# Two due steps of the attention heads for one weight piece, in a two-layer hybrid trunk

## The chip, the cores and the metric

One Trainium2 chip, one core. The metric is the device time of one execution in microseconds (us), the median of several runs; lower is better. PE is TensorE, DVE is VectorE, ACT is ScalarE, POOL is GpSimd, SP is SyncE, which here only issues DMAs.

## What is computed

Two layers over a sequence of 256 frames of width 2048, all in float32. Each layer projects `x` with one wide matrix, feeds three groups of heads, gates them, and maps them back:

```python
def hybrid_layer(x, mem, w_in, rel_table, gate_w, gate_b, gla_norm_g, w_mem_kv, w_out, ln_g, ln_b):
    h = x @ w_in
    a_q, a_k, a_v, a_z, b_q, b_k, b_v, b_z, b_lr, m_q, m_z = jnp.split(h, cuts, axis=-1)
    y_a = chunk_band_attention(a_q, a_k, a_v, rel_table)      # 8 heads of 128, own chunk of 64 and 8 before
    log_g = jax.nn.log_sigmoid(b_lr @ gate_w + gate_b) / GATE_TAU
    o_b = gla_chunk_recurrence(b_q, b_k, b_v, log_g)          # 4 heads, gated linear attention
    o_b = o_b * lax.rsqrt(mean(o_b ** 2) + RMS_EPS) * gla_norm_g
    mk, mv = jnp.split(mem @ w_mem_kv, 2, axis=-1)
    y_m = memory_attention(m_q, mk, mv)                       # 4 heads into 256 memory tokens
    y = jnp.concatenate([y_a * silu(a_z), o_b * silu(b_z), y_m * silu(m_z)], axis=-1)
    return layer_norm(DEEPNORM_ALPHA * x + y @ w_out, ln_g, ln_b)
```

## The kernel before

**The weight stream.** Nearly all the work is the product of the 256 frames with the weights, which are streamed once from HBM. A product of 512 output columns is a group (`as_group`, L266) of eight weight *pieces*, each of 256 rows. A piece (`piece`, L140) is loaded by SP into `raw`; ACT casts it to `wh` (L128) and DVE forms the rest `wl` (L129), four buffers of each; PE then makes 12 matmuls of a piece into the tile `acc`: `xh*wh`, `xl*wh`, `xh*wl` for two blocks of rows and two of frames. Groups come in this order in a layer: (MV, MK), BQK, two groups of values (512 and 264 columns), AQ0, AK0, values (512), AQ1, AK1, values (264), MQ, BZ, AZ0, AZ1, MZ, and four of the output projection (WO0 and WO1 in turns, WO2, WO3).

**The steps beside it.** The heads are Python generators whose `yield n` means "not before `n` more ticks". After each piece `tick` (L52) moves the clock on by the piece's width (1 for 512 columns, 0.516 for 264) and decides what is issued behind that piece. It first runs all due entries of `side` (reads back of turned tiles, splits, gating), and then works on `active`: up to two head generators while the recurrence `gla` runs, up to three afterwards, drawn from `waiting`. A generator that ends does not count; one that yields again ends the tick. `finish` ticks on, without weight pieces, until given generators are done.

- `gla` (L306): the linear attention of one layer, thirteen steps, the only one of its kind.
- `a_head` (L540), heads a0 to a7: first step two score matmuls into a bank of PSUM, softmax on DVE (`L547`, `L552`, `L555`, `L557`) and ACT (`L554`), turning by `turned`; `yield 9`; second step the products with the values (from `asv`), copy to `yraw` by ACT (`L590`); `yield 2`; end. Heads 0 to 3 also load the bias of head h + 4 in the second step. For heads 0, 1 and 7 the turned scores `pT` and the values are first split into two parts (`split`, on ACT and DVE), into tiles whose buffers carry the tags `gq` or `gk` and `pairs0` or `pairs1`; the tiles `yT` of `gla_turned` use `gq` and `gk` too.
- `m_head` (L593), heads m0 to m3: scores against the memory keys, softmax (`L607`, `L608`, `L611` to `L614`), turning; `yield 10`; split of `pT`; `yield 2`; products with the values; `yield 2`; end.
- `turned` (L520): DVE transposes blocks into a scratch tile, POOL stores it in DRAM (`home`, L527), and two ticks later POOL issues four reads back (L532).
- `gated` (L499): when all heads of a group are done, their outputs are multiplied with the SiLU gate and split, as an operand of the output projection.

PE, SP and POOL issue in the order in which the program is written, so the tick decides what stands between which pieces in their queues. On DVE and ACT the order is set when the program is built, by a list scheduler with priorities (the weight casts and `wl` go ahead by a high priority) and a model of the times; `placed_here` pins an instruction behind the one written before it on its engine. PSUM has four banks for the steps (`bank`), the scratch pool has eight tiles.

Of the kernel before, what the change touches and what calls it, by code (L numbers as in the profile page):

```python
# [36 lines left out]
def hybrid_trunk_kernel(  # L37
# [14 lines left out]
    def tick(share=1.0):  # L52

        now[0] += share
        for e in [e for e in side if e[1] <= now[0]]:
            side.remove(e)
            after = next(e[0], None)
            if after is not None:
                side.append((e[0], now[0] + after))
            else:  # L60
                done.add(e[0])
        while True:
            while waiting and len(active) < (3 if all(g in done for g in linear) else 2):
                active.append((waiting.pop(0), 0))
            due = [e for e in active if e[1] <= now[0]]
            if not due:
                return
            active.remove(due[0])
            g = due[0][0]
            after = next(g, None)  # L70
            if after is not None:
                active.append((g, now[0] + after))
                return
            done.add(g)

    def finish(gens):
        while not all(g in done for g in gens):
            tick()
# [187 lines left out]
    def as_group(src, xq, n, kp=2, first=None, need={}):  # L266

        acc = psd.tile([P, 2, 512], F32, name=nm("acc"), tag="acc")
        for pc in range(16 // kp):
            if first is not None and pc % 2 == 0:  # L270
                xq.append(load_quarter(first[pc // 2]))
            finish(need.get(pc, ()))
            w = piece(src[pc], n, kp)
            for kk in range(kp):
                for t in range(2):
                    as_products(acc[:, t, :n], t, xq, w, pc * kp + kk, kk)
            tick(n / 512)
        return acc
# [558 lines left out]
    for l in range(L):  # L837
# [176 lines left out]
        for n in range(WO_N):  # L1014
# [35 lines left out]
            for m, pc in order:  # L1050
                finish(need.pop(pc, ()))
                w = piece(wo_pieces(l, m)[pc], 512)
                for kk in range(2):
                    for t in range(2):
                        as_products(accs[m][:, t], t, yq, w, pc * 2 + kk, kk)
                tick()
                if pc == 7:
                    for t in range(2):
                        add_residual(m, t, accs[m][:, t], stats)
                    if last:  # L1060
                        r = res[:, 1, columns(m)]
                        dve.tensor_tensor(r, r, gb[m][0], op=ALU.mult)
# [97 lines left out]
```

## Time and profile before

| | |
|---|---|
| median of 3 runs | 897.69 us (896.99 to 899.18) |
| span of the profiled execution | 896.4 us, 13888 instructions; it is this span that stands for the profiled execution's own time |
| PE busy | 887.2 us, 99% |
| DVE, ACT, POOL busy | 617.4 us, 482.1 us, 231.0 us |
| granted PE clock | 0.997 on average |
| DMA | 216.90 MB, mean 242 GB/s |

Times within the profile are counted from the span's start. A row of the chain has start, duration, engine, output tile and line; a row of a timeline has the engine, the line, the operation, the tiles and shapes, and in brackets the idle time of the engine before it with what ended it. Rows of matmuls that overlap give the time from the first start to the last modelled end. A row of windows gives the busy time of PE, PE's weight load, DVE, ACT and POOL, the granted clock, the share of the DMA engines and GB/s. In a row of waits stand the total, the number and the longest.

### The profile page before, as it was taken

How to read it: one execution, taken by the hardware profiler on the slowest of the kernel's cores; microseconds unless marked ns; L12 is line 12 of the kernel's file. 1: busy time of each engine (PE TensorE's matmuls, PEld its weight loads, DVE VectorE, ACT ScalarE, POOL GpSimd, SP SyncE). 2: the span in 40 equal slices, each digit the busy share in tenths (PEclk: the TensorE clock that was granted, in tenths of full speed). 3: DMA queues.
4: the chain of work that ended last, by engine and by line, in shares of the span. 5: the costliest groups of instructions: out<-in, count | busy, mean ns of one | idle time of the engine just before them, and what ended most of it. 6: DMA issues, size and time to landing. Idle time of an engine off the chain costs nothing.

```text
span 896.4 us, 13888 instructions
## 1 busy us (share of the span) xinstructions
PE 887.2 (99%) x4669; PEld 743.5 (83%) x4669; DVE 617.4 (69%) x905; ACT 482.1 (54%) x698; POOL 231.0 (26%) x431
## 2 busy tenths in 40 slices
PE   9999999999999999999999999999999999999996
PEld 7878988888988888888888888888888888888885
DVE  6756568767467676665595786896664758676866
ACT  6644475555446575543465545754754557565440
POOL 0022103114305353410034230231061444432300
PEclk9999999999999999999999999999999999999998
DMA  9988779867979797975689968696589897979752
GB/s 310 312 241 245 215 245 265 275 197 225 275 253 241 236 274 236 307 241 193 224 267 268 265 195 282 201 287 210 154 234 293 242 260 236 276 222 281 223 179 95
DMA packets 166088, 216.90 MB, mean 242 GB/s; under 512 B 25232, under 2 KB 143376, under 8 KB 166016
## 3 DMA queue, kind: packets, MB, share of 16 engines
q1 hardware_dynamic: 148256, 173.29, 63.7%
q0 software_dynamic: 17472, 42.33, 16.4%
q8 instruction: 37, 0.61, 0.3%
q10 hardware_dynamic: 288, 0.39, 0.1%
q14 instruction: 35, 0.29, 0.1%
HBM read 194.78 MB, written 21.10 MB: 241 GB/s over the span
## 4 chain that ended last, share of the span: by engine, by line
PE 98%; DVE 1%; DMA 0%; ACT 0%; issue 0%; SPq 0%; DVEq 0%
PE acc L102 91%; PE bk L102 6%; DMA raw<-w 0%; ACT wh L128 0%; DVE mv L129 0%; ACT res L823 0%; DVE wl L129 0%; PE bk L665 0%; DVE stats L809 0%; DVE res L808 0%; SPq L201 0%; DVE res L759 0%; SPq L179 0%; DVE mvt L762 0%; PE bk L812 0%
## 5 line engine op out<-in xcount | busy, mean ns | idle before, releaser
L102 PE MATMUL acc<-wh,x 128*128 128x512 f32 (+2 forms) x2516 | 747.8, 381 | 1.3 <-DVE mv L129 0.7
L102 PEld LDWEIGHTS acc<-wh,x 128*128 128x128 f32 x2516 | 460.6, 188 | 88.2 <-PE acc L102 1.1
L129 DVE TENSOR_TENSOR wl<-raw,wh 128x1024 fp32r<-128x1024 f32 (+3 forms) x321 | 368.4, 1152 | 198.9 <-ACT wh L128 187.0
L128 ACT CAST wh<-raw 128x1024 fp32r<-128x1024 f32 (+3 forms) x321 | 318.5, 996 | 344.2 <-PE acc L102 201.7
L102 PE MATMUL acc<-wl,x 128*128 128x512 f32 (+2 forms) x1258 | 475.9, 379 | 0.0
L102 PEld LDWEIGHTS acc<-wl,x 128*128 128x128 f32 x1258 | 236.0, 188 | 45.3 <-DVE wl L129 0.4
L527 POOL DMA_DIRECT2D home<-sc x76 | 42.5, 560 | 426.2 <-DVE sc L525 417.6
L532 POOL DMA_DIRECT2D pT<-home x96 | 52.4, 552 | 30.2 <-DMA home<-sc 12.1
L532 POOL DMA_DIRECT2D qk<-home x64 | 34.9, 553 | 36.5 <-DMA home<-sc 26.2
L532 POOL DMA_DIRECT2D zT<-home x48 | 26.2, 551 | 20.5 <-DMA home<-sc 14.0
L525 DVE STREAM_TRANSPOSE sc<-sc 128x512 f32<-128x512 f32 (+1 forms) x38 | 24.9, 668 | 3.7 <-ACT sc L996 3.0
L532 POOL DMA_DIRECT2D yr<-home x48 | 26.3, 557 | 3.2 <-DMA home<-sc 3.2
L525 DVE STREAM_TRANSPOSE sc<-acc 128x512 f32<-128x512 f32 x28 | 18.3, 691 | 4.3 <-PE acc L102 4.3
L554 ACT ACTIVATE sc<-sc,mx 128x128 f32<-128x128 f32 (+1 forms) x32 | 14.3, 448 | 8.9 <-DVE mx L552 8.8
L547 DVE SCALAR_TENSOR_TENSOR sc<-bk,bias 128x384 f32<-128x384 f32 x16 | 8.6, 539 | 10.7 <-PE bk L102 10.7
L128 ACT CAST x<-sc 128x512 fp32r<-128x512 f32 x20 | 12.2, 617 | 5.2 <-DVE sc L508 3.2
L532 POOL DMA_DIRECT2D xT<-home x24 | 13.2, 552 | 6.9 <-DMA xT<-home 5.2
L129 DVE TENSOR_TENSOR x<-sc,x 128x512 fp32r<-128x512 f32 x20 | 13.5, 685 | 1.4 <-ACT x L128 1.4
L102 PE MATMUL bk<-qk,qk 128*128 128x128 f32 (+1 forms) x64 | 13.1, 326 | 0.0
L698 DVE SCALAR_TENSOR_TENSOR res<-res,acc 128x512 f32<-128x512 f32 x15 | 9.7, 682 | 4.7 <-PE acc L102 4.7
L532 POOL DMA_DIRECT2D yT<-home x16 | 8.8, 555 | 14.8 <-DMA home<-sc 14.8
L129 DVE TENSOR_TENSOR x<-res,x 128x512 fp32r<-128x512 f32 (+2 forms) x13 | 10.0, 790 | 2.0 <-ACT x L128 2.0
(210 smaller groups left out, 524.3 us busy)
## 6 DMA issues: line engine op xcount, KB each, us to landing
raw<-w SPq DMA_DIRECT2D x387, 256.0 KB, 4.6
raw<-w SPq DMA_DIRECT2D x62, 512.0 KB, 5.0
home<-sc POOLq DMA_DIRECT2D x60, 256.0 KB, 4.4
raw<-w SPq DMA_DIRECT2D x32, 388.0 KB, 5.1
raw<-w SPq DMA_DIRECT2D x32, 264.0 KB, 3.5
qk<-home POOLq DMA_DIRECT2D x64, 64.0 KB, 4.7
raw<-w SPq DMA_DIRECT2D x32, 124.0 KB, 4.8
bias<-relw SPq DMA_DIRECT2D x16, 192.0 KB, 4.4
```

The lines of the kernel that those rows point to most:

```text
L102: pe.matmul(o, l, r, start=start, stop=stop, skip_group_check=True)
L128: keep(act.copy(hi, src))
L129: keep(dve.tensor_tensor(lo, src, hi.bitcast(F32), op=ALU.subtract))
L525: dve.transpose(blocks.rearrange(order, j=32), src.rearrange("p (g b j) -> p g b j", b=4, j=32))
L527: pool.dma_start(homes[-1], blocks)
L532: pool.dma_start(dst[b * 32:(b + 1) * 32], home[:, b].rearrange("(a i) n -> i a n", a=4))
L547: dve.scalar_tensor_tensor(s, pb[:, :384], SCALE, bias[h], op0=ALU.mult, op1=ALU.add)
L554: act.activation(s[:, own[t]], s[:, own[t]], AF.Exp, bias=mx[:, t:t + 1], accum_out=zs[:, t:t + 1])
L698: dve.scalar_tensor_tensor(r, r, ALPHA, acc, op0=ALU.mult, op1=ALU.add)
```

## The change

In `tick`, a head step that yields again no longer ends the tick; the second one does.

```diff
             else:
                 done.add(e[0])
+        steps = 0
         while True:
             while waiting and len(active) < (3 if all(g in done for g in linear) else 2):
                 active.append((waiting.pop(0), 0))
...
             after = next(g, None)
             if after is not None:
                 active.append((g, now[0] + after))
-                return
+                steps += 1
+                if steps == 2:
+                    return
+                continue
             done.add(g)
```

The limits of `active`, all due times, the weight pieces and the work of every step stay as they are.

## The prediction

> **What bounds the kernel now.** I read the page first (engine shares, slices, the chain that ended last), then the waits of TensorE (PE), then the chain piece by piece, and only then the clock times of single heads.
>
> ```profile
> PE 887.2 (99%) x4669; PEld 743.5 (83%) x4669; DVE 617.4 (69%) x905; ACT 482.1 (54%) x698; POOL 231.0 (26%) x431
> PE   9999999999999999999999999999999999999996
> PEclk9999999999999999999999999999999999999998
> PE acc L102 91%; PE bk L102 6%; DMA raw<-w 0%; ACT wh L128 0%; DVE mv L129 0%; ACT res L823 0%; DVE wl L129 0%; PE bk L665 0%; DVE stats L809 0%; DVE res L808 0%; SPq L201 0%; DVE res L759 0%; SPq L179 0%; DVE mvt L762 0%; PE bk L812 0%
> ...
> PE bk L102 <- DVE eps L836: 1.1, 1, 1.1
> PE bk L812 <- DVE nt L777: 0.9, 1, 0.9
> PE acc L102 <- DVE mv L129: 0.7, 1, 0.7
> PE acc L102 <- ACT wh L128: 0.7, 2, 0.3
> PE bk L102 <- ACT nparts L813: 0.3, 1, 0.3
> ```
>
> The chain is PE for 97%: 91% weight products (acc), 6% matmuls of the heads and the transposes (bk). The second block is every wait of PE: 3.7 us in all, and by the names they lie at the start (eps, mv) and in the last normalization (nt, nparts); none belongs to a head. So where the change acts PE never waits, at full clock. In such a kernel a new order gains only what a change-over between two kinds of matmul costs, and loses whatever makes PE wait.
>
> ```profile
> 240.90 21.80 PE acc L102 x96
> 262.69 0.66 PE bk L102 x4
> ...
> 292.64 0.65 PE bk L102 x4
> 293.29 2.75 PE acc L102 x12
> 296.05 0.65 PE bk L102 x4
> ```
>
> The chain in order of time (start, duration). Eight pieces without a step take 21.80 us: 2.725 us a piece, 0.227 us a matmul. With a step between, a piece and its step take 296.05 - 292.64 = 3.41 us: 0.65 the step's own four matmuls, 0.035 the change-over.
>
> **The change part by part.** *Which ticks change.* I counted through the ticks by the yields (9 and 2 in an attention head; 10, 2, 2 in a memory head; the recurrence's own list), with one step and with two. They differ, in each layer, in six ticks that now let two through: scores of a1 and a2 behind AQ1's last piece; products with the values ("values" below) of a1 and a2 behind the second 264-column piece; scores of a4 and a5 (BZ, first piece); values of a4 and a5 (AZ0, second); scores of a7 and m0 (AZ0, fourth); m1's split and m2's scores (AZ1, seventh). Of these the first five put two matmul groups side by side. What follows moves up too: a5 and a6 by one piece, a7 by one, m0 and m1 by two, m2 by five, m3 by three, the last gating by two. The recurrence is due alone at its ticks, and no loop of empty ticks gets shorter.
>
> *PE's own work.* No matmul is added or taken. Ten pairs (five in each of two layers) save at most one change-over each: 10 x 0.035 = 0.35 us, at least nothing. I take 0.2, between the two.
>
> *First scores, SP and the banks.* The 16 bias loads stay; a2's second load (for a6) is issued two short pieces earlier, 192 KB that then stand ahead of two weight loads in SP's queue. Weights have their smallest reserve just behind that place:
>
> ```profile
> 234.11 1.23 DVE L129 TENSOR_TENSOR wl<-raw,wh 128x1024 fp32r<-128x1024 f32 x1 [1.83 <-ACT wh L128]
> 237.80 0.40 PE L102 MATMUL acc<-wl,x 128*128 128x512 f32 x1
> 220.00:242.00 22.00, 22.00 (x148) 20.39 (x147) 10.60 (x15) 10.62 (x17) 12.05 (x23) 1.00 0.94 273
> ```
>
> The rest of a weight piece is ready at 235.34 and used at 237.80: 2.46 us. 192 KB at the 273 GB/s of that stage are 0.70 us. Cost 0 under that cover; without it up to 0.7 us a layer.
>
> *a2, a5, a6.* Their values come up to two short pieces (a matmul of 264 columns by 0.227 x 264/512 = 0.117, so 2 x 12 x 0.117 = 2.8 us) or one long one earlier, but their scores move up as well.
>
> ```profile
> 223.39 1.18 POOL L532 DMA_DIRECT2D pT<-home  x2 [0.62 <-DMA yr<-home]
> DMA to landing us min/median/max: 3.4/4.3/5.7
> 230.82 0.81 PE L102 MATMUL bk<-pT,asv 128*128 128x256 f32 x4
> ```
>
> The middle row is the time from issue to landing of the pT reads of that stage (min, median, max). a2's last read is issued at about 224.0 and lands by 228.3 (median) to 229.7; PE needs it at 230.82, afterwards at 228.0. On POOL the order becomes home a1, home a2, reads a1, reads a2, then eight reads for the queries (AQ1), which today stand ahead of a2's and take 4.4 us: a2 gains more than the 2.8 it loses. The query reads are late by a2's four (2.2 us), with eight pieces of cover. Cost 0.
>
> *m0 and m1 scores* at about 297.3 and 300.8 need the memory queries:
>
> ```profile
> 280.44 0.69 DVE L129 TENSOR_TENSOR mq<-yr,mq 128x512 fp32r<-128x512 f32 x1
> 302.71 0.76 PE L102 MATMUL bk<-mk,mq 128*128 128x256 f32 x5
> 303.32 2.26 POOL L532 DMA_DIRECT2D yT<-home  x4 [4.28 <-DMA home<-sc]
> 310.77 0.56 POOL L527 DMA_DIRECT2D home<-sc  x1 [4.64 <-DVE sc L525]
> ```
>
> Ready at 281.1: cover 16 us. But m0's store (home), 8.1 us after its scores today, now stands on POOL ahead of the reads of yT, the recurrence's output: these go from 303.3 to about 305.9 and are used by ACT at 317.86 (below). Even landing 5.7 us late they have over 4 us left. Cost 0.
>
> *a7's values* are the tight place.
>
> ```profile
> 317.86 1.28 ACT L495 ACTIVATE x<-yT,ng 128x128 fp32r<-128x128 f32 x4
> 319.15 1.13 DVE L496 SCALAR_TENSOR_TENSOR x<-yT,ng,x 128x128 fp32r<-128x128 f32 x4
> 320.31 0.41 ACT L128 CAST sc<-pT 128x256 fp32r<-128x256 f32 x1 [0.23 <-DVE x L496]
> 322.30 0.71 ACT L128 CAST sc<-pT 128x256 fp32r<-128x256 f32 x2 [0.43 <-DMA pT<-home]
> 321.67 0.28 DVE L129 TENSOR_TENSOR sc<-asv,sc 128x128 fp32r<-128x128 f32 x1
> 321.90 1.23 DVE L129 TENSOR_TENSOR wl<-raw,wh 128x1024 fp32r<-128x1024 f32 x1
> 323.05 0.76 DVE L129 TENSOR_TENSOR sc<-pT,sc 128x256 fp32r<-128x256 f32 x2
> 325.99 0.52 PE L102 MATMUL bk<-sc,sc 128*128 128x256 f32 x3
> 765.94 0.52 PE L102 MATMUL bk<-sc,sc 128*128 128x256 f32 x3
> ```
>
> a7's split shares a buffer (tag gk) with yT, so it starts only when VectorE (DVE) has done with yT at 320.28, whatever its due time, and ends at 321.95. PE uses it at 325.99 today, at 325.99 - 2.72 = 323.27 afterwards: the reserve falls from 4.0 to 1.3 us. (The last row is the same step in layer 1, 439.95 us on.) m0's split moves up two pieces and could come first: 0.71 on ACT, 0.76 on DVE. That still fits. Cost 0; at the other end one weight piece gets ahead on DVE as well, 0.76 + 1.23 - 1.32 = 0.7 us a layer. I take 0, nearer to the order of today's rows.
>
> The Trainium skill, TensorE: Matmul & The Clock Gate, section on engine queue depths, says that matmuls stay in program order and that ScalarE and VectorE are strict FIFO. It speaks against the change: a step let through before its data is there holds up every weight piece behind it. Here that would be the whole 0.7 us a layer, since the trace has no idle PE time in which to make it good; in today's order no step of a head shows it.
>
> *m1's values.*
>
> ```profile
> 332.97 1.08 ACT L996 ACTIVATE sc<-acc 128x512 f32<-128x512 f32 x2
> 333.94 0.71 ACT L128 CAST sc<-pT 128x256 fp32r<-128x256 f32 x2
> 335.47 0.72 DVE L129 TENSOR_TENSOR sc<-pT,sc 128x256 fp32r<-128x256 f32 x2
> 340.98 0.89 PE L102 MATMUL bk<-sc,mv 128*128 128x256 f32 x6
> 347.37 1.28 ACT L611 ACT_TABLE_LOAD   x1 [1.83 <-DVE mx L608]
> ```
>
> m1's split ends at 336.19, PE uses it at 340.98: 4.8 us. Afterwards two pieces less and m2's scores more (0.72) precede: 340.98 - 5.44 + 0.72 = 336.26. Its reads and its split are issued two pieces (5.4 us) earlier as well, so the reserve stays if the split keeps its distance to its reads. If it stays behind AZ1's SiLU (332.97, itself 0.72 later) there is none: rival two. m2 and m3 give their values in WO with the same 12 ticks after their scores as now. I take 0.
>
> *Sum.* Against the profiled span of 896.4: -0.2 + 0 = 896.2. The runs are 896.99, 897.69 and 899.18; the median is 1.3 us above that span. Forecast 897.69 - 0.2 = 897.5, no change. A measurement of this kernel tells about 0.3%, 2.7 us, from none.
>
> **The rivals.** *One: a7's split is late.* 0.7 us in each layer gives 897.5 + 1.4 = 898.9. For it: a reserve of 1.3 us, and ACT and DVE are busiest just there. Against: m0's split alone does not fill it. It would pass 0.3% only at 1.4 us a layer, two more weight pieces.
>
> *Two, slower: m1's split stays behind the SiLU.* m2's exponentials now fall ahead of that SiLU, so ScalarE must load the exponential's table and then the SiLU's again. Split ended at 336.19 + 0.72 = 336.91 against a need of 336.26: 0.65 us late with no load, 1.93 with one of 1.28, 3.2 with two. At two layers 1.3, 3.9 or 6.4 us: 898.8, 901.4, 903.9; with one load the middle, 901.4. It decides from one load on. For it: the split stands behind the SiLU today although its reads were issued by 322.4. Against: it is two pieces earlier in program order, and ACT has idle time before the SiLU.
>
> The Trainium skill, ScalarE: Activation LUTs, section on what a table load costs, gives about 1283 ns and a drain of some 1380 ns for each switch. The trace agrees on the load, 1.28 us; no row here prices the drain. By the page's total a late split with one load costs an estimated 2 x 1.38 = 2.8 us more, 904.2.
>
> *Three, faster: side by side the second group hides under the first.* If all of it went, 10 x 0.65 = 6.5 us, 891.2. Against: the 96 plain matmuls above are neighbours of one kind already and still take 0.227 us each; neighbours do not hide under one another.
>
> *Four: the change does nothing.* Only 12 ticks let two through; the time is then 897.7, inside the forecast.
>
> **How the numbers follow.** Forecast (with four) 0.63, rival one 0.21, two 0.13, three 0.03. Predicted 897.5. From 896.3 (0.35 saved, the lower runs' 0.7 below the median, a little over) to 901.5 (rival two with one load); outside lie rival three and the upper part of two, together with mixtures no more than 2 in 10. The forecast's own range is 896.3 to 899.2. Faster by over 0.3%: rival three, 0.03. Slower: most of two and 0.01 of one, 0.11. Within: 0.86.
>
> **What would show it.** Right: no wait of PE on a head's split, pT or mq; busy PE near 887 us; in the chain ten pairs of head steps as one entry of about 1.3 us; a7's values near 323.3 and 763.2 with idle PE ahead of them at most some tenths. Wrong: a wait "PE bk L102 <- DVE sc L129" (rival one near 323 and 763, two near 336 and 776), more than today's table loads, or a wait of PE on wl or wh near 237. A reordering of casts by the planner elsewhere, which the rows of before can't show, would also make it wrong.

## The result and the profile after

The changed kernel takes 900.8 us (median), the kernel before, beside it, 898.08 us: ratio 1.003, interval 1.0022 to 1.0039. It is slower by 2.7 us; the forecast was no change. Measured again beside other experiments, it gave 1.0031 (1.0019 to 1.0043). Each ratio here is taken against the kernel before as run beside it (its median there 897.87 to 898.29 us) and is not exactly the quotient of the medians. One of the twelve executions with only the pairs of a4 and a5 took 1275.73 us at a mean clock of 0.655; that run's numbers are given without it.

The profiled execution (902.17 us, span 900.3) is the second longest of thirteen; one part of its loss is not usual, as an experiment shows below. The page's row of engines and the first row of PE's waits after the change:

```profile
PE 890.2 (99%) x4669; PEld 745.0 (83%) x4669; DVE 616.4 (68%) x905; ACT 488.2 (54%) x702; POOL 231.7 (26%) x431
PE bk L106 <- DMA pT<-home: 2.6, 3, 1.4
```

(Line numbers are four higher than before.) The wait is new: 2.6 us in all, three times, 1.4 the longest, on `pT`, the turned scores that a head reads back from DRAM. None of the waits that the rivals named is there. PE's timeline around the values of a4 and a5 shows where, first before the change (layer 0), then after it (two rows of each layer); the brackets hold the idle time ahead of a row:

```profile
289.07 0.81 PE L102 MATMUL bk<-pT,asv 128*128 128x256 f32 x4
292.48 0.81 PE L102 MATMUL bk<-pT,asv 128*128 128x256 f32 x4
```

```profile
288.60 0.81 PE L106 MATMUL bk<-pT,asv 128*128 128x256 f32 x4
290.24 0.89 PE L106 MATMUL bk<-pT,asv 128*128 128x256 f32 x4 [0.83 <-DMA pT<-home]
...
729.97 0.89 PE L106 MATMUL bk<-pT,asv 128*128 128x256 f32 x4 [0.35 <-DMA pT<-home]
732.24 1.31 PE L106 MATMUL bk<-pT,asv 128*128 128x256 f32 x4 [1.39 <-DMA pT<-home]
```

a5's values now stand directly behind a4's, at 289.2 and not 3.41 us later, and its turned scores are not there: 0.83 us in layer 0, 1.39 in layer 1, where a4's are late as well (0.35). POOL's timeline of the same stretch says why: first before the change, then after it. A row is a run of transfers that POOL issues; `home` is a head's store to DRAM, `yr` the eight reads for the memory queries (MQ), `pT` the reads of turned scores.

```profile
267.99 0.54 POOL L527 DMA_DIRECT2D home<-sc  x1 [5.81 <-DVE sc L525]
268.54 4.45 POOL L532 DMA_DIRECT2D yr<-home  x8
273.24 0.56 POOL L527 DMA_DIRECT2D home<-sc  x1 [0.25 <-DVE sc L525]
273.80 0.55 POOL L532 DMA_DIRECT2D pT<-home  x1
275.40 1.69 POOL L532 DMA_DIRECT2D pT<-home  x3 [1.05 <-DMA yr<-home]
277.08 0.56 POOL L527 DMA_DIRECT2D home<-sc  x1
279.43 2.17 POOL L532 DMA_DIRECT2D pT<-home  x4 [1.79 <-DMA home<-sc]
```

```profile
267.54 0.54 POOL L531 DMA_DIRECT2D home<-sc  x1 [5.81 <-DVE sc L529]
273.45 0.54 POOL L531 DMA_DIRECT2D home<-sc  x1 [5.37 <-DVE sc L529]
274.02 4.37 POOL L536 DMA_DIRECT2D yr<-home  x8
278.89 0.56 POOL L531 DMA_DIRECT2D home<-sc  x1 [0.51 <-DMA yr<-home]
279.45 1.10 POOL L536 DMA_DIRECT2D pT<-home  x2
281.05 2.26 POOL L536 DMA_DIRECT2D pT<-home  x4 [0.50 <-DMA yr<-home]
283.88 1.64 POOL L536 DMA_DIRECT2D pT<-home  x3 [0.58 <-DMA yr<-home]
285.78 0.55 POOL L536 DMA_DIRECT2D pT<-home  x1 [0.26 <-DMA pT<-home]
287.27 1.09 POOL L536 DMA_DIRECT2D pT<-home  x2 [0.94 <-DMA pT<-home]
```

Before, POOL used the time between a4's store and a5's store for the MQ reads. Now a5's scores stand behind the same weight piece as a4's, so in program order a5's store comes directly behind a4's, ahead of the MQ reads. The store is not earlier for it: DVE still works through a4's softmax before a5's, and a5's store starts at 273.45 (273.24 before). DVE's first instruction on a5's scores shows it; it starts when a4's are turned:

```profile
266.67 0.58 DVE L529 STREAM_TRANSPOSE sc<-sc 128x384 f32<-128x384 f32 x1
267.17 0.52 DVE L551 SCALAR_TENSOR_TENSOR sc<-bk,bias 128x384 f32<-128x384 f32 x1
```

So POOL stands 5.37 us, and then issues all it has in one burst. a4's four reads end up 5 us later (279.45 to 281.6 for 273.80 to 276.5).

The reserve of a5 in layer 0 can be worked out from these rows and one of the chain after the change, which follows the wait back to the transfer:

```profile
284.42 5.68 DMA pT<-home
290.10 0.14 issue
290.24 0.89 PE bk L106 x4
...
719.75 6.21 DMA home<-sc
725.97 0.28 issue
726.25 5.86 DMA pT<-home
732.11 0.14 issue
732.24 1.31 PE bk L106 x4
733.55 3.95 PE acc L106 x12
```

Before, a5's fourth read was issued at 279.43 + 3 x 0.54 = 281.05 and landed at 286.33 by the record of its semaphore; PE used it at 292.48: a reserve of 6.15 us. After, it goes out at 284.42 and lands at 290.10, 3.77 us later (3.37 by the issue, 0.40 by a slower landing). PE would use it 0.65 us behind the start of a4's values, at 289.25, which is 3.23 us earlier. 6.15 - 3.77 - 3.23 = -0.85 us; the idle time measured is 0.83.

In layer 1 the last row shows a second effect: twelve matmuls in 3.95 us, which normally take 2.75. The windows of that stretch (length, busy PE, PEld, DVE, ACT and POOL with the number of their instructions, the granted clock, the share of the DMA engines, GB/s):

```profile
732.00:734.00 2.00, 1.76 (x6) 1.58 (x7) 0.39 (x1) 0.37 (x1) 0.77 (x2) 0.64 0.77 202
734.00:736.00 2.00, 2.00 (x6) 1.52 (x6) 0.00 (x0) 0.00 (x0) 0.00 (x0) 0.51 0.83 277
```

PE, idle for 1.7 us between 729.6 and 732.2, got half the clock afterwards; the clock records of the trace put it at 732.57 to 735.98, 3.41 us, which is 1.7 us of work. Waits of 2.6 and 1.7 make 4.3 us; the spans differ by 3.9.

### The profile page after: what moved, and what is told of

The parts are those of the page before. It is cut to its first block, busy times and chain, and to the rows that moved or that the text cites. A ratio compares the mean times of both kernels' runs of the same rounds, so it can differ in the third digit from the quotient of the medians.

```text
span 900.3 us, 13883 instructions
## 1 busy us (share of the span) xinstructions
PE 890.2 (99%) x4669; PEld 745.0 (83%) x4669; DVE 616.4 (68%) x905; ACT 488.2 (54%) x702; POOL 231.7 (26%) x431
## 4 chain that ended last, share of the span: by engine, by line
PE 81%; issue 9%; DMA 6%; POOL 2%; DVE 1%; ACT 0%; POOLq 0%; ACTq 0%
PE acc L106 76%; PE bk L106 5%; DMA home<-sc 2%; DMA qk<-home 1%; DMA pT<-home 1%; POOL pT L536 1%; POOL yr L536 1%; DMA yr<-home 1%; POOL home L531 0%; DMA raw<-w 0%; POOL kdT L536 0%; ACT wh L132 0%; DVE wl L133 0%; ACT res L827 0%; PE bk L669 0%
## 5 line engine op out<-in xcount | busy, mean ns | idle before, releaser
L106 PE MATMUL bk<-pT,asv 128*128 128x128 f32 (+1 forms) x52 | 10.8, 328 | 2.6 <-DMA pT<-home 2.6
L106 PEld LDWEIGHTS bk<-pT,asv 128*128 128x128 f32 x52 | 9.1, 194 | 4.3 <-issue 2.3
```

Of the source, the lines that this page charges most:

```text
L106: pe.matmul(o, l, r, start=start, stop=stop, skip_group_check=True)
```

## The experiments

The theory: the six ticks of the prediction are harmless but for the group a4, a5, a6. Scores of a4 and a5 behind one piece bring POOL into the worse order, values of a4 and a5 behind one piece need the result earlier, and only together do they use up the reserve. Rivals: another pair costs the time; one of the two halves alone is enough; the half clock is the loss, not the wait.

**One step per piece in BZ alone.** With the scores of a4 and a5 their values too come one by one; the pairs of a1 and a2 stay, and a7's scores join a6's values instead of m0's scores. `marks` holds the tick at which a layer's BZ begins.

```diff
-                if steps == 2:
+                if steps == (1 if marks and 0 < now[0] - marks[-1] <= 8 else 2):
```

> Two steps are let through everywhere but behind the pieces of BZ, where a4, a5 and a6 give their scores one by one as before. Theory (late landing): the loss sits in the values of a4 and a5, whose turned scores land late because a5's store stands on POOL ahead of the eight reads for the memory queries, and whose need is a piece earlier. Here both are as before, so PE has no wait on pT, and the time is that of the kernel before within 0.1%: ratio 0.999 to 1.001, though four of the six pairs of each layer are still made. Rival (the other moves: m0 to m3 earlier, four more table loads on ACT): a loss of some 2 us stays, ratio 1.002 to 1.003.

897.41 us, ratio 0.9995 (0.9986 to 1.0004). No wait on `pT`. The pairs of a1 and a2, that of a7 and the memory heads that move up (m0 and m1 by a piece here) cost nothing that can be measured; the whole loss hangs on the scores of a4 and a5 being let through together, with all that follows from it.

**Only the pairs of a4 and a5** (scores behind BZ's first piece, values behind AZ0's second), no other pair of the change. a6, a7, m0 and m1 move up one piece behind them.

```diff
-                if steps == 2:
+                if steps == (2 if marks and now[0] - marks[-1] in (1, 9, 10, 11) else 1):
```

> One step a tick everywhere but behind BZ's first piece and behind the second to fourth of AZ0: only the pair a4 and a5 is let through together, in scores and in values. Theory: the whole loss, ratio 1.002 to 1.004, with PE waits on pT of 2 to 3 us in all. Rival (the other moves cost): ratio 0.999 to 1.001.

900.15 us, ratio 1.0020 (1.0010 to 1.0031). Its wait on `pT` is the longest row of its waits; the profiled execution, 903.25 us, is the longest of the eleven:

```profile
PE bk L107 <- DMA pT<-home: 3.7, 2, 2.4
```

These pairs alone bring the loss (the interval overlaps with that of the whole change), by the same wait.

**Late reads without the earlier need**: the scores stay together, the values of a4, a5 and a6 come one by one, each as late as before.

```diff
-                if steps == 2:
+                if steps == (1 if marks and 8 < now[0] - marks[-1] <= 12 else 2):
```

> Two steps everywhere but behind the first four pieces of AZ0: scores of a4 and a5 in one tick, their values in two as before. Theory: the landing stays late (POOL's order is the changed one), but a5 is needed 2.7 us later again, which covers its lateness of 0.8 and 1.4 us; a4's own 0.35 us in layer 1 may stay. Ratio 0.999 to 1.001, PE's wait on pT under 0.5 us in all. Rival (lateness from the scores' side alone, the transfers clash whatever the need): the wait stays over 1.5 us, ratio 1.002 to 1.003.

898.78 us, ratio 1.0007 (0.9995 to 1.0018). POOL's order is that of the changed kernel (a5's last two reads are the first two of the last row here), and PE uses a5 without a wait. The profiled execution (897.57 us) is one of the shortest of eleven, which reach to 902.02; whether a wait stands in the longer ones no profile here shows:

```profile
273.21 0.54 POOL L532 DMA_DIRECT2D home<-sc  x1 [5.38 <-DVE sc L530]
273.77 4.37 POOL L537 DMA_DIRECT2D yr<-home  x8
...
283.72 2.25 POOL L537 DMA_DIRECT2D pT<-home  x4 [0.73 <-DMA yr<-home]
```

```profile
291.77 0.81 PE L107 MATMUL bk<-pT,asv 128*128 128x256 f32 x4
```

**The earlier need without late reads**: the kernel before, in which a5's values alone are due a piece earlier and join a4's.

```diff
+        steps = 0
...
-                return
+                steps += 1
+                if steps == (2 if marks and now[0] - marks[-1] == 10 else 1):
+                    return
+                continue
...
-        yield 9
+        yield 8 if h == 5 else 9
```

> The kernel before with its one step per piece, except that a5's values are due one piece earlier and let through together with a4's, behind AZ0's second piece. POOL's order is as before: home a4, eight reads for the memory queries, home a5, reads a4, home a6, reads a5, reads a6. Of the two things that the change does to a5 (store and reads later on POOL, values a piece earlier on PE) this is the second alone. Theory: either alone is covered. a5's reads land at about 287.5 in layer 0 (four issued from 282.24 in 2.17 us, 4.0 to 5.3 us to landing), the need falls to about 289.3: no wait of PE on pT over 0.3 us, ratio 0.999 to 1.001, span 896 to 897. Rival: the earlier need alone uses up the reserve, since the reads of a5 always landed just in time: a wait on pT of 1 to 2 us in each layer, and a half clock behind it in layer 1, ratio 1.002 to 1.004.

897.93 us, ratio 1.0001 (0.9992 to 1.0009). Both heads' values in one go, no wait:

```profile
289.98 1.47 PE L107 MATMUL bk<-pT,asv 128*128 128x256 f32 x8
```

So late reads alone cost nothing that can be measured, earlier need alone nothing, both together about 0.2 to 0.3%. That is the theory's square in two halves: late reads alone stand beside the changed kernel (0.9995 to 1.0018 against 1.0022 to 1.0039), earlier need alone beside the run with only the pairs of a4 and a5 (0.9992 to 1.0009 against 1.0010 to 1.0031).

**POOL in another order, all pairs kept**: the MQ reads, and the reads of a4 and a5, one tick earlier, so that POOL issues MQ reads, a4's and a5's stores, their reads, and a6's store behind them.

```diff
-        side.append((reads(), now[0] + 2))
+        side.append((reads(), now[0] + back))
...
-        turned(96, (pT, s))
+        turned(96, (pT, s), back=1 if h in (4, 5) else 2)
...
+            return q, staged(G_MQ, xq, yraw[3], place, back=1)
```

> All pairs of the change stay, on PE too; only POOL's queue is reordered: the reads of the memory queries come a tick earlier (ahead of a4's store), those of a4 and a5 a tick earlier (ahead of a6's store). Theory (the head of POOL's queue): a5's reads are issued by about 280.2 instead of 284.4 in layer 0 and land by 286, 3 us ahead of their need at 289.2; no wait of PE on pT, ratio 0.999 to 1.001. Rival (two heads' transfers crowd the DMA engines): time to landing stays at 5.5 us against 4.7 and the wait at over 1.5 us, ratio 1.002 to 1.003.

902.82 us, ratio 1.0051 (1.0034 to 1.0067): worse, where it was to be cured. The waits of a4 and a5 are gone in both layers, but one of a6 has come in layer 1:

```profile
721.95 0.56 POOL L531 DMA_DIRECT2D home<-sc  x1 [1.58 <-DVE sc L529]
730.09 2.18 POOL L536 DMA_DIRECT2D pT<-home  x4 [7.57 <-PE acc L106]
```

```profile
736.42 0.89 PE L106 MATMUL bk<-pT,asv 128*128 128x256 f32 x4 [2.75 <-DMA pT<-home]
```

Half clock follows here too (737.44 to 740.85), and five of the six executions show a mean clock of 0.995 or 0.996. In the changed kernel a6's reads start just as late (730.04) and land at 736.37 by their semaphore; there a5's wait and the half clock had moved a6's use back to 737.34. So the new order did not make a6 late: it took away the wait that had hidden it.

**The same order, and a6's values two pieces later.**

```diff
-        yield 9
+        yield 11 if h == 6 else 9
```

> All pairs of the change, POOL issuing the reads of the memory queries first and those of a4 and a5 ahead of a6's store (as in the run with the reordered POOL), and a6's values two pieces later, which moves a7 and the memory heads later by up to two pieces too. Theory: that run had no wait on a4 or a5 left and lost only because a6's reads came 2.7 us late in layer 1; two pieces are 5.4 us, so a6's wait goes as well. No wait of PE on pT over 0.5 us, no half clock, ratio 0.999 to 1.001, span 896 to 897.5: the pairs cost nothing once POOL's order fits them, and gain next to nothing. Rival: something else in the pairs costs time beside the late reads (colliding softmaxes on DVE, or weight pieces held up by them); then the ratio stays at 1.002 or above with no wait on pT. What could also go wrong: a7 or the memory heads, now later, run into the normalization or the output projection and cost there.

897.95 us, ratio 1.0000 (0.9991 to 1.0008), no wait on `pT` left, as the theory said. So the pairs themselves cost nothing once their transfers are in time, and gain nothing that can be measured either.

**a5's values one piece later, all else as changed.**

```diff
-        yield 9
+        yield 10 if h == 5 else 9
```

> The changed kernel with one due time altered: a5's products with the values are due ten pieces after its scores, not nine. All pairs of scores stay, a4 and a5 behind BZ's first piece among them, and so does POOL's late order (home a4, home a5, eight reads for the memory queries, home a6, reads a4, reads a5). Theory: the late landing of a5 alone is covered where the need is as late as before; a5's wait goes. a4's reads are late by 5.6 us against the kernel before with its need unchanged: its wait of up to 0.4 us in layer 1 can stay. Waits on pT at most 0.5 us in all, ratio 0.999 to 1.001. Rival: the late order costs time by itself, since each read on POOL also stands behind the landing of the eighth before it; then a wait on pT of a4 or a6 over 1 us takes its place, ratio 1.002 or more.

899.55 us, ratio 1.0028 (1.0015 to 1.0041): the theory's number missed. The profiled execution (898.5 us, the shortest of seven, which reach to 903.52) shows a5 in time and a6 directly behind it late:

```profile
291.57 0.81 PE L106 MATMUL bk<-pT,asv 128*128 128x256 f32 x4
293.00 0.89 PE L106 MATMUL bk<-pT,asv 128*128 128x256 f32 x4 [0.62 <-DMA pT<-home]
```

a6's reads are late by POOL's order too and its need is still a piece early; in the changed kernel a5's wait hid that. Whether a6's wait is longer in the longer executions no profile here shows.

**PE kept busy ahead of a5's values**, to tell the wait from the half clock. The matmuls add 1.1 us of PE work a layer.

```diff
+            if h == 5:
+                for _ in range(5):
+                    mm(po[:, :P], ident, ident, True, True)
```

> The changed kernel as it is, with five plain 128x128 matmuls of the identity (0.22 us each, 1.1 us a layer) put ahead of a5's products with the values; their result is overwritten and not used. Theory: the loss in layer 1 has two parts, the wait itself (0.35 + 1.39 us) and the half clock that follows it (3.41 us at half speed, 1.7 us of work lost). With PE kept busy for 1.1 us of the wait the idle time before a5's values falls to 0.3 us and the clock stays at 1.00 behind it: the chain's entry of twelve matmuls behind a5's values is 2.75 us again and not 3.95, and the loss against the kernel before falls from 2.7 to about 1.2 us, ratio 1.0013, with a span near 898. In layer 0, where the wait is 0.83 us, up to 0.3 us are added. Rival: the clock fell for another reason than PE's idle time (the load of the whole core at that place); then the half clock is seen again at 732 to 736 us and the ratio stays at 1.003.

901.68 us, ratio 1.0044 (1.0031 to 1.0058). The clock stayed at 1.00, as expected, but the loss did not shrink: the ratio and the span (900.0 us) missed what was expected. In layer 0 the matmuls filled a5's wait. In layer 1 the wait fell ahead of them, on a4, and they came on top:

```profile
731.38 0.89 PE L106 MATMUL bk<-pT,asv 128*128 128x256 f32 x4 [1.05 <-DMA pT<-home]
732.11 1.28 PE L106 MATMUL bk<-ident 128*128 128x128 f32 x10
733.23 0.82 PE L106 MATMUL bk<-pT,asv 128*128 128x256 f32 x4
```

A further 0.29 us of waiting stands ahead of a6's values. Waits of 1.3 us and 2.2 us of added matmuls make 3.5; the span is 3.6 us over that before. The run therefore says little on what the half clock is worth; the next one says more.

**The changed kernel once more.**

> The changed kernel once more, unaltered: of the thirteen executions the profiled one was the second longest (span 900.3 us, clock 0.996), and only the two longest show a clock below 0.997. Theory: the half clock of 3.41 us is no part of the usual loss; a usual execution loses its 2.7 us by the waits on the turned scores of a4 and a5 alone. A profile of an execution with a clock of 0.997 or more then shows the order of POOL unchanged, waits of PE on pT of 2 to 3.5 us over the two layers, the clock at 1.00 in 728 to 742 us, and a span of 898 to 899.5. Rival: the half clock is the larger part; then an execution without it shows waits of at most 1.2 us and a span under 897.5. The ratio should come out at 1.002 to 1.004 again.

901.15 us, ratio 1.0031 (1.0019 to 1.0043), and the profiled execution has no half clock in these stretches (the total of the wait, a5's two rows, and the clock's windows):

```profile
PE bk L106 <- DMA pT<-home: 3.8, 3, 2.1
...
291.53 0.89 PE L106 MATMUL bk<-pT,asv 128*128 128x256 f32 x4 [1.15 <-DMA pT<-home]
733.62 0.89 PE L106 MATMUL bk<-pT,asv 128*128 128x256 f32 x4 [2.06 <-DMA pT<-home]
```

```profile
732.00:734.00 2.00, 0.38 (x2) 0.38 (x3) 1.67 (x2) 0.04 (x1) 1.53 (x3) 1.00 0.50 117
734.00:736.00 2.00, 2.00 (x12) 1.67 (x11) 0.00 (x0) 0.37 (x1) 0.00 (x0) 1.00 0.84 241
```

Its span is 900.0 us, 3.6 over that before, against 3.8 us of waits on `pT`. 3.2 of them are a5's. The remaining 0.54 is ahead of a3's values in layer 0 (240.51): there a3's last read landed at 240.37 by its semaphore, in the first profile at 235.66, before the change at 235.42. So the ticks of a1 and a2 left a3 in time in one execution and not in another; what made it late no run here shows. The waits and the span lie a little above what was expected for a usual execution (3.5 and 899.5); it is the longest of its five. Of the eighteen executions of the changed kernel only two have a mean clock under 0.997, the two longest of the first thirteen. So the loss does not need the half clock, which is an addition in some; that the waits alone make the usual 2.7 us is likely but not shown, as both profiles are of long executions.

## Why the prediction was wrong

By the steps of the prediction:

- *What bounds the kernel*: right. PE is busy 99% of the span before and after, and what made PE wait was lost. The sentence taken there from the Trainium skill, TensorE: Matmul & The Clock Gate, that matmuls stay in program order (the page has it in Part 2, Step-by-step: what each phase is for), fits: while a5's `pT` was missing, 0.83 and 1.39 us, PE ran no weight piece either.
- *Which ticks change*: right. In layer 1 the scores of a1 and a2, their values, and the scores of a4 and a5 are one entry of the chain each, near the 1.3 us forecast (a1's values have five matmuls), and so are a7 and m0 (1.37 us, ten matmuls); the values of a4 and a5 are parted by the wait:

```profile
640.60 1.31 PE bk L106 x8
...
667.93 1.23 PE bk L106 x9
...
703.10 1.31 PE bk L106 x8
```

- *PE's own work*: 0.2 us gained cannot be told from nothing: the kernel with all pairs and no wait has 1.0000 (0.9991 to 1.0008).
- *First scores, SP and the banks*: right, no new wait of PE on `wl` or `wh` near 237.
- ***a2, a5, a6*: this step failed.** It worked the order on POOL out for a2 (home a1, home a2, reads a1, reads a2, then the queries' reads) and put "Cost 0" to all three. For a5 the same way of counting gives home a4, home a5, eight MQ reads, home a6, reads a4, reads a5, reads a6: the MQ reads, which were done between two stores, now stand behind the second, and POOL waits 5.37 us for it with all the reads of heads behind. And the sentence that the scores move up as well was true of PE only: a5's store did not move, since DVE takes the heads one after the other. The rows for it were in the trace of before, the POOL rows above: store 273.24, released by DVE with 0.25 us to spare, and eight reads ahead of it. The term, put at 0, is 0.83 us in layer 0 and 1.74 in layer 1 of the first profile, 1.15 and 2.06 in the second.
- *m0 and m1 scores*, *a7's values* (rival one): right. a7's split ended at 321.16 and PE used it at 323.79 (323.27 was forecast), without a wait.
- *m1's values* (rival two): four more table loads on ACT came, as that rival said (702 instructions on ACT for 698; 26 loads for 22, by the groups), but m1's split moved ahead of them (CAST at 324.98) and PE did not wait for it. They cost nothing that can be measured. A wait on a memory head's split, 0.52 us, came only in two of the experiments, with the values of a4 and a5 one by one and with a5's one piece later (output projection of layer 1, near 808).
- The time, 900.8 us, lies within the range by luck, through a mechanism that no rival had; the 0.86 for "within 0.3%" rested on the step above. A loss was named as a wait on the split (DVE `sc`) or the weights; a wait on `pT` was named only as what a right forecast would not show.

## What to carry to other kernels

When a step is let through earlier, write out the order of every queue that it feeds for each such step, not for one of them, and ask for each store what releases it: an in-order queue waits at it, and what comes behind is late though it was not moved. A reserve is spent from both ends; here either half of the change (landing 3.8 us later, need 3.2 us earlier) was covered by 6.15 us, and both were not. A repair of the order has to be followed to the next head in the queue: a wait that is taken away can lay bare the one it hid.

## What the runs showed of the hardware

- In this program POOL's transfers complete on eight semaphores in turn: in the trace's records (numbers 110 to 117) each transfer waits until the eighth before it has landed. The brackets in POOL's rows after the change are of this kind: the reads from 281.05, 283.88, 285.78 and 287.27 wait for `yr` and `pT` transfers, eight places ahead. In layer 1 the chain above shows it end to end: a6's store (719.75, 6.21 us to landing) holds a5's fourth read (726.25). At 5 to 6 us of landing no more than eight are under way, so a burst does not go out at POOL's 0.54 us apiece.
- The half clock comes in steps of 3.413 us: the clock's stretches are whole multiples (727.04 us are 213 of them, 160.43 are 47). Laid on that raster, the windows ahead of a drop in the weight stream were idle for 0.51 (changed kernel, 729.15 to 732.57) and 0.70 (reordered POOL, 734.02 to 737.44) of their length. The wait of 2.06 us in the repeated run fell across two windows (0.39 and 0.21) and that of 2.36 in the run of a4 and a5 alone likewise (0.26 and 0.43), and the clock stayed. So a wait's price depends on where it lies on the raster; in the weight stream these runs leave the boundary between 0.43 and 0.51. It is no general rule: at the end of the run with the reordered POOL and a6 later, where transposes and matmuls of 8 rows run, the clock fell behind a window idle for 0.38 (887.28 to 890.69) by the same count. The Trainium skill, TensorE: Matmul & The Clock Gate, section on the HAM clock gate, gives a free-running window of 3413 ns, which agrees, and an idle window as what lowers the clock; here a window idle for half was enough.
- Open: in layer 1 POOL begins a6's first read 3.09 us after the last wait of its own that the records show, and it does so in all eleven profiles, the kernel before among them (722.20 to 725.29; changed kernel 726.95 to 730.04; reordered POOL 727.00 to 730.09). In layer 0 the same step takes 0.51 us where POOL waited (before, 281.73 to 282.24; reordered POOL, 285.72 to 286.22). So it is not the change's doing, but in the reordered run it is about as long as the wait of a6 (2.75 us). Nothing in the records explains it, and no run here looked for its cause.
